# Two transfers on GpSimd's queue behind the first pair of its sums, in a gated two-layer MLP with seven-product matmuls

## Chip, cores and metric

One core of one Trainium2 chip. The metric is device time in microseconds (us), the median of several executions; lower is better. "Set" is a quarter of the tokens (1024 of 4096); the kernel works through four sets one after the other. A "chunk" is 128 of the 2048 columns of the hidden layer; each of the sums S1 to S4 of g has eight chunks.

## The reference

```python
x: 16 x 256 x 512, w1: 512 x 4096, w2: 2048 x 512      # float32
h = x @ w1
gate, value = np.split(h, 2, axis=-1)
h = np.maximum(gate, 0) * value
return (h @ w2).astype(np.float32)
```

## The kernel before

Both matmuls are done as seven products of 2x2 blocks instead of eight. That needs sums of the operands: T1 to T4 of the weights, S1 to S4 of x and of the gated hidden layer g.

Accumulating and casting transfers are issued by GpSimd, each with one helper (cut, comments added):

```python
SUMS = (("S1", "A21", "A22", SUB), ("S2", "S1", "A11", SUB), ("S4", "A12", "S2", ADD), ("S3", "A11", "A21", SUB))

def add_w2(m, v):
    nc.gpsimd.dma_start(out=V[m], in_=V[v], accum_op=ADD)

def cast_x(s):                       # x of set s to 16 bits, in DRAM; DMA transposes read it later
    nc.gpsimd.dma_start(out=x16[s], in_=x2[s * SET:(s + 1) * SET, :])

def g_sum(eng, go, n, h0, h1):       # chunks h0 to h1 of sum n, by engine eng
    for m, i0, i1, op in SUMS:
        if m == n:
            eng.tensor_tensor(go[n][:, h0:h1], go[i0][:, h0:h1], go[i1][:, h0:h1], op=op)
```

GpSimd's work in the first set, in its order (cut, comments added):

```python
for t in TURNS:
    w1_one(nc.gpsimd, 12, 4, *t)
    if t[0] == "T2":
        add_w2("T1", "B12")
add_w2("T3", "B22")
add_w2("T2", "T1")                   # must wait until T1 has landed
cast_x(1)
...
    if n == "P2" and s == 0 and jb in (11, 13, 15):
        h = jb - 11                  # 0, 2, 4
        if h == 4:
            add_w2("T4", "T2")       # must wait until T2 has landed
        for m in ("S1", "S3")[:2 - h // 4]:
            g_sum(nc.gpsimd, go, m, h, h + 2)
```

So GpSimd makes two pairs (S1 and S3 of chunks 0 to 1, then 2 to 3) and one last sum, S1 of chunks 4 to 5. What is left is VectorE's after the set's last block (cut):

```python
        if s == 0:
            g_sum(nc.vector, go, "S1", 6, 8)
            for m in ("S2", "S4"):
                for h in (0, NHC // 2):
                    g_sum(nc.vector, go, m, h, h + NHC // 2)
            g_sum(nc.vector, go, "S3", NHC // 2, NHC)
```

TensorE reads them right after, in the products P5 (S1), P6 (S2), P3 (S4), P7 (S3). VectorE's next work in its order is two evictions each of P3 and P7 (an eviction takes a finished product out of the memory in which TensorE adds up), the four sums of the next set's x, eight sums of w1 and then the evictions of the second half.

Of the kernel before, what the change touches and what calls it, by code (L numbers as in the profile page):

```python
# [29 lines left out]
@with_exitstack  # L30
def kernel(ctx: ExitStack, tc: tile.TileContext, x, w1, w2, out):






    nc = tc.nc
    x2 = x.flatten_outer_dims()
    out2 = out.flatten_outer_dims()  # L40
    flagpool = ctx.enter_context(tc.tile_pool(name="flagpool", bufs=1))
    flag = flagpool.tile([1, 1], dt.int32, name="flag")
    with ExitStack() as fast:
        unfit = fast_way(fast, tc, x2, w1, w2, out2, flag)
    with tc.If(unfit > 0, label="general"):
        with ExitStack() as general:
            general_way(general, tc, x2, w1, w2, out2)
# [52 lines left out]
def fast_way(ctx, tc, x2, w1, w2, out2, flag):  # L100
# [54 lines left out]
    def w1_ops(eng, jb, n):  # L155
        for t in TURNS:
            w1_one(eng, jb, n, *t)

    def w1_one(eng, jb, n, m, a, b, o):
        eng.tensor_tensor(W(m, jb, n), W(a, jb, n), W(b, jb, n), op=o)  # L160

    def add_w2(m, v):
        nc.gpsimd.dma_start(out=V[m], in_=V[v], accum_op=ADD)
# [12 lines left out]
    def x_tiles():  # L176
        o = {f"A{h}": xpool.tile([P, 4, TH], F16, name=f"x_A{h}") for h in (1, 2)}
        for h in (1, 2):
            for k in (1, 2):
                o[f"A{h}{k}"] = o[f"A{h}"][:, 2 * k - 2:2 * k]  # L180
        for n in ("S1", "S2", "S3", "S4"):
            o[n] = xpool.tile([P, 2, TH], F16, name=f"x_{n}")
        return o
# [88 lines left out]
    def g_sum(eng, go, n, h0, h1):  # L272
# [3 lines that stand above are left out]
# [69 lines left out]
    def advance(stream, n):  # L345
        for _ in range(n):
            if stream is None or next(stream, 0) == 0:
                return
# [5 lines left out]
    def fetch_w2(i):  # L354
        ks, n = slice(i // 2 * NHC, i // 2 * NHC + NHC), i % 2
        nc.gpsimd.dma_start(out=w2_h[n][:, ks], in_=w2_v[:, ks, n * HALF:(n + 1) * HALF])

    def cast_x(s):
        nc.gpsimd.dma_start(out=x16[s], in_=x2[s * SET:(s + 1) * SET, :])

    def g_tiles():
        g = gpool.tile([P, NJ, SET], F16, name="g")
        gs = {n: gpool.tile([P, NHC, TH], F16, name=f"g_{n}") for n in ("S1", "S2", "S3", "S4")}
        return g, g_ops(g, gs)
# [21 lines left out]
    def turn_by_dma(s, o, h):  # L386
        for k in range(2):
            nc.sync.dma_start_transpose(out=o[f"A{h + 1}{k + 1}"], in_=x16[s][h * TH:(h + 1) * TH, k * 256:k * 256 + 256])
# [7 lines left out]
    def fetch_rows(s, q):  # L396
        rows[s, q] = xpool.tile([P, 2, D], F16, name=f"xn{q % 2}")
        nc.sync.dma_start(out=rows[s, q], in_=x16[s][q * 256:(q + 1) * 256].rearrange("(b p) d -> p b d", p=P))
# [50 lines left out]
    def x_sum(o):  # L449
        n, i0, i1, op = sums.pop(0)  # L450
        nc.vector.tensor_tensor(o[n], o[i0], o[i1], op=op)
# [64 lines left out]
    for s in range(NS):  # L516
        if s:
            g, go = g_tiles()
        first = NPLAIN if s == 0 else 0
        blocks = {jb: Block(xo, g, jb) for jb in range(first, NJ)}  # L520
        if s == 0:
            blocks[first] = lead
        plan = {jb * PERIOD + at: (jb, n) for jb in blocks for n, at in SLOT.items() if (s, jb, n) != (0, first, "P1")}
        last = NJ * PERIOD
        stream = mm2_stream(s, go)
        if s == 0:
            w1_ops(nc.gpsimd, 4, 2)
            fetch_w2(0)
            fetch_w2(1)
            w1_ops(nc.gpsimd, 6, 2)  # L530
            fetch_w2(2)
            fetch_w2(3)
            w1_ops(nc.gpsimd, 8, 2)
            w1_ops(nc.gpsimd, 10, 2)
            for to, v in ((V["T1"], V["B11"]), (v_12, w2_h[1]), (V["T4"], V["B21"])):
                nc.sync.dma_start(out=to, in_=v)
            for t in TURNS:
                w1_one(nc.gpsimd, 12, 4, *t)
                if t[0] == "T2":
                    add_w2("T1", "B12")  # L540
            add_w2("T3", "B22")
            add_w2("T2", "T1")
            cast_x(1)
        for at in range(first * PERIOD, last + PERIOD):
            if at in plan:
                jb, n = plan[at]
                if n == "P1" and s and jb in (4, 8):
                    fetch_rows(s, 1 + jb // 4)
                if n == "P2" and s == 0 and jb in (11, 13, 15):
                    h = jb - 11  # L550
                    if h == 4:
                        add_w2("T4", "T2")
                    for m in ("S1", "S3")[:2 - h // 4]:
                        g_sum(nc.gpsimd, go, m, h, h + 2)
                getattr(blocks[jb], n)()
                ended = jb - (n == "P7") if n == "P7" or (n, jb) == ("P4", NJ - 1) else -1
                if ended in blocks:
                    blocks[ended].finish()
                if n == "P5":
                    for f in LOOKS.get((s, jb), ()):  # L560
                        f()
                if ended >= 0 and s:
                    if ended < NHC:
                        g_sum(nc.gpsimd, go, "S3", ended, ended + 1)
                        if s == 1 and ended in (1, 4):
                            cast_x(2 + ended // 4)
                    elif ended < NJ - BY_DVE:
                        for m in ("S1", "S2", "S4"):
                            g_sum(nc.gpsimd, go, m, ended - NHC, ended - NHC + 1)
            elif at >= last:  # L570
                advance(stream, 4)
            else:
                advance(prev, 4)
# [6 lines that stand above are left out]
        else:  # L580
            for m in ("S1", "S2", "S4"):
                g_sum(nc.vector, go, m, NHC - BY_DVE, NHC)
        done = 20
        if s + 1 < NS:
            xo = x_tiles()
            for h in range(2):
                turn_by_dma(s + 1, xo, h)
            for q in range(2):
                fetch_rows(s + 1, q)
            advance(stream, 100)  # L590
            sums = list(SUMS)
            for _ in SUMS:
                x_sum(xo)
            if s == 0:
                w1_ops(nc.vector, 0, 2)
                w1_ops(nc.vector, 2, 2)
            advance(stream, MM2 - TAIL - 100 - done)
        else:
            advance(stream, MM2)
        prev = stream  # L600
# [29 lines left out]
```

## Time and profile before

| | before |
|---|---|
| time, median of 3 | 311.59 us (311.24 to 311.88) |
| profiled span | 309.5 us |
| TensorE busy | 301.5 us (97%) |
| GpSimd busy | 148.0 us (48%) |
| TensorE idle outside start and end | 0.74 us by the records, all between 66 and 74 us |

The "busy" of an engine is the time in its instructions. In the rows in order of time that follow, the columns are start, duration, engine, line, operation, output and inputs, count, and in brackets the idle time of the engine just before and what ended it. TensorE's matmul ends are modelled and overlap the next start, so gaps are best taken from starts. The lines that carry the reading stand in the prediction.

### The profile page before, as it was taken

What the parts mean: (1) busy time and instruction counts of PE and PEld (TensorE: products, weight loads), DVE (VectorE), ACT (ScalarE), POOL (GpSimd) and SP (SyncE); (2) the same over time, 40 slices, a digit from 0 to 9 for tenths busy, and PEclk for the clock granted to TensorE, in tenths of its full rate; (3) what the DMA queues carried; (4) which work ended last, traced back from release to release, by engine and by line L of the source; (5) the groups of instructions that cost most, each with busy time, mean ns of one, the idle gap of its engine ahead of it and who ended that gap; (6) DMA issues with size and microseconds to landing.
All of it is one profiled execution on the core that took longest, in us unless ns stands there. A gap on an engine that the chain in (4) does not pass through costs nothing.

```text
span 309.5 us, 5081 instructions
## 1 busy us (share of the span) xinstructions
PE 301.5 (97%) x1859; PEld 181.9 (59%) x1859; DVE 217.0 (70%) x330; ACT 188.8 (61%) x450; POOL 148.0 (48%) x135
## 2 busy tenths in 40 slices
PE   7999999999999999999999999999999999999994
PEld 4554444578854444478874444458884444447883
DVE  1477888898548888884338888886526888888401
ACT  3357766547577667648847667656857666673230
POOL 5779996950003437992001435995000434899000
PEclk9999999999999999999999999999999999999999
DMA  7999979998314370055221010028311101000113
GB/s 250 203 203 204 224 198 215 204 120 238 120 68 102 71 169 0 3 95 159 87 102 37 34 34 2 0 48 156 140 71 68 34 2 34 0 2 0 69 68 140
DMA packets 33450, 30.74 MB, mean 99 GB/s; under 512 B 13873, under 2 KB 27953, under 8 KB 33201
## 3 DMA queue, kind: packets, MB, share of 16 engines
q0 software_dynamic: 10704, 11.54, 23.0%
q1 hardware_dynamic: 22576, 18.75, 20.6%
q8 instruction: 15, 0.25, 0.3%
q10 hardware_dynamic: 144, 0.13, 0.1%
q14 instruction: 11, 0.08, 0.1%
HBM read 24.12 MB, written 11.53 MB: 115 GB/s over the span
## 4 chain that ended last, share of the span: by engine, by line
PE 92%; DVE 2%; ACT 2%; DMA 1%; issue 1%; SPq 0%; DVEq 0%
PE Y L202 25%; PE X L202 16%; PE W L202 16%; PE Y L286 13%; PE W L286 8%; PE X L286 8%; PE X L259 2%; PE W L259 2%; DMA g<-in_w_dram 1%; DVE g_S L275 1%; ACT x_A L377 0%; ACT v L264 0%; ACT x_A L384 0%; PE W L375 0%; DVE g L241 0%
## 5 line engine op out<-in xcount | busy, mean ns | idle before, releaser
L275 POOL TENSOR_TENSOR g_S<-g 128x512 f16<-128x512 f16 (+1 forms) x47 | 60.0, 1300 | 125.3 <-DVE g L241 123.3
L202 PEld LDWEIGHTS <-wt 128*128 128x128 f16 x480 | 47.0, 98 | 55.3 <-issue 0.6
L202 PE MATMUL Y<-x_S,wt 128*128 128x512 f16 x240 | 71.4, 379 | 0.0
L202 PE MATMUL X<-x_A,wr 128*128 128x512 f16 x240 | 71.4, 379 | 0.0
L202 PEld LDWEIGHTS <-wr 128*128 128x128 f16 x360 | 35.2, 98 | 40.7 <-issue 0.2
L229 DVE SCALAR_TENSOR_TENSOR cc<-W,pu 128x512 f32<-128x512 f32 x60 | 41.5, 692 | 23.6 <-ACT pu L223 23.5
L209 ACT COPY Y<-X 128x512 f32<-128x512 f32 x60 | 34.2, 571 | 37.5 <-PE X L202 37.0
L286 PEld LDWEIGHTS <-g_S 128*128 128x128 f16 x512 | 49.9, 98 | 7.0 <-DVE g_S L275 1.3
L235 DVE SCALAR_TENSOR_TENSOR cc<-Y,pu 128x512 f32<-128x512 f32 x60 | 41.5, 691 | 6.4 <-PE Y L202 0.4
L223 ACT ACTIVATE pu<-Y 128x512 f32<-128x512 f32 x60 | 35.8, 597 | 14.2 <-PE Y L202 14.2
L230 DVE SCALAR_TENSOR_TENSOR g<-X,cc 128x512 f16<-128x512 f32 x60 | 41.5, 691 | 2.3
L286 PEld LDWEIGHTS <-g 128*128 128x128 f16 x384 | 37.5, 98 | 8.2
L241 DVE SCALAR_TENSOR_TENSOR g<-Y,cc 128x512 f16<-128x512 f32 x60 | 40.9, 681 | 1.8 <-PE Y L202 1.8
L216 ACT ACTIVATE pu<-W 128x512 f32<-128x512 f32 x60 | 36.1, 602 | 0.3 <-PE W L202 0.3
L202 PE MATMUL Y<-x_A,wt 128*128 128x512 f16 x120 | 35.7, 379 | 0.1
L202 PE MATMUL W<-x_S,wr 128*128 128x512 f16 x120 | 35.7, 379 | 0.0
L202 PE MATMUL W<-x_S,wt 128*128 128x512 f16 x120 | 35.7, 379 | 0.0
L286 PE MATMUL X<-w,g 128*128 128x256 f16 x256 | 31.2, 273 | 0.0
L286 PE MATMUL Y<-v,g_S 128*128 128x256 f16 x256 | 30.7, 273 | 0.4 <-DVE g_S L275 0.4
L316 DVE SCALAR_TENSOR_TENSOR o<-W,pv 128x256 f32<-128x256 f32 x16 | 6.8, 423 | 30.3 <-PE W L286 30.3
L275 POOL TENSOR_TENSOR g_S<-g,g_S 128x512 f16<-128x512 f16 x18 | 21.8, 1211 | 1.4
L275 POOL TENSOR_TENSOR g_S<-g_S,g 128x512 f16<-128x512 f16 x18 | 21.4, 1187 | 1.4
(69 smaller groups left out, 294.7 us busy)
## 6 DMA issues: line engine op xcount, KB each, us to landing
out_dram<-o SPq DMA_DIRECT2D x16, 256.0 KB, 2.1
out_dram<-pv SPq DMA_DIRECT2D x15, 256.0 KB, 2.0
x<-in_x_dram POOLq DMA_DIRECT2D x3, 1024.0 KB, 8.1
xn<-x SPq DMA_DIRECT2D x12, 256.0 KB, 3.3
wr<-in_w_dram POOLq DMA_DIRECT2D x4, 512.0 KB, 14.4
w<-in_w_dram POOLq DMA_DIRECT2D x4, 512.0 KB, 11.9
wr<-in_w_dram POOLq DMA_DIRECT2D x6, 256.0 KB, 8.4
g_S<-in_x_dram SPq DMA_DIRECT2D x2, 512.0 KB, 4.6
```

The lines of the kernel that those rows point to most:

```text
L202: nc.tensor.matmul(ps, W(wn, self.jb)[:, b], self.xo[xn][:, b, :], start=fresh and b == 0, stop=b == 1, skip_group_check=True)
L209: nc.scalar.copy(out=self.Y, in_=self.X)
L216: nc.scalar.activation(self.p5, self.W, COPY, scale=GS)
L223: nc.scalar.activation(self.u2, self.Y, COPY, scale=-GS)
L229: nc.vector.scalar_tensor_tensor(out=self.c12, in0=self.W, scalar=GS, in1=self.u2, op0=MULT, op1=ADD)
L230: nc.vector.scalar_tensor_tensor(out=self.g[:, self.jb, :TH], in0=self.X, scalar=0.0, in1=self.c12, op0=MAX, op1=MULT)
L235: nc.vector.scalar_tensor_tensor(out=self.c22, in0=self.Y, scalar=-GS, in1=self.p5, op0=MULT, op1=ADD)
L241: nc.vector.scalar_tensor_tensor(out=self.g[:, self.jb, TH:], in0=self.Y, scalar=0.0, in1=self.c22, op0=MAX, op1=MULT)
L259: nc.tensor.matmul(ps[:, ts], W(name, self.jb)[:, e % 2], a[:, e, ts], start=e == 0, stop=e == 3, skip_group_check=True)
L275: eng.tensor_tensor(go[n][:, h0:h1], go[i0][:, h0:h1], go[i1][:, h0:h1], op=op)
L286: nc.tensor.matmul(ps, go[gn][:, k, b * P:(b + 1) * P], V[vn][:, k, :], start=fresh and k == 0, stop=k == NHC - 1, skip_group_check=True)
L316: nc.vector.scalar_tensor_tensor(out=d["o1"][:, HALF:], in0=d["W"], scalar=1 / GS, in1=d["pu"][:, 1], op0=MULT, op1=ADD)
```

## The change

Its intent: GpSimd stood waiting for T1 to land, ahead of the T2 transfer, while sums that it could have made were ready. T2 and the cast of x go behind the first pair of sums.

```diff
             add_w2("T3", "B22")
-            add_w2("T2", "T1")
-            cast_x(1)
...
                     for m in ("S1", "S3")[:2 - h // 4]:
                         g_sum(nc.gpsimd, go, m, h, h + 2)
+                    if h == 0:
+                        add_w2("T2", "T1")
+                        cast_x(1)
```

## The prediction

> **What bounds the kernel now.** I read the page's busy shares first, then the row of tenths, the chain that ended last inside the stretch that the change touches, and last the instructions of GpSimd, VectorE and TensorE there in order of time.
>
> The page, parts 1 and 2:
>
> ```profile
> PE 301.5 (97%) x1859; PEld 181.9 (59%) x1859; DVE 217.0 (70%) x330; ACT 188.8 (61%) x450; POOL 148.0 (48%) x135
> ...
> PE   7999999999999999999999999999999999999994
> ```
>
> TensorE is busy 301.5 of 309.5 us, so whatever GpSimd does, all that can be won is the 8 us in which TensorE is idle. Most of that is the first and the last slice (the table of stretches has 2.46 us in the first 10 us, 3.9 us in the last 29), which this change doesn't touch. The same table, cut finer between 62 and 78 us (columns: stretch, length, then busy us and count for PE, PEld, DVE, ACT, POOL, then clock, DMA share, GB/s), has the only other hole of any size:
>
> ```profile
> 64.00:66.00 2.00, 2.00 (x21) 1.80 (x19) 2.00 (x1) 1.01 (x3) 1.82 (x1) 1.00 0.97 168
> 66.00:70.00 4.00, 3.61 (x34) 3.01 (x32) 4.00 (x5) 2.73 (x7) 0.00 (x0) 1.00 1.43 149
> 70.00:74.00 4.00, 3.65 (x34) 3.04 (x33) 3.23 (x5) 3.23 (x7) 0.00 (x0) 1.00 0.95 185
> 74.00:78.00 4.00, 4.00 (x39) 3.57 (x38) 3.65 (x7) 2.78 (x6) 0.00 (x0) 1.00 0.90 321
> ```
>
> Note also "2.00 (x1)" of VectorE in 64 to 66: one instruction fills it. The chain of waits there leaves TensorE for VectorE's sums (L275) just after the first set's last block:
>
> ```profile
> 63.11 0.70 DVE g L241
> ...
> 66.44 1.00 issue
> 67.43 3.50 DVE g_S L275 x3
> 70.93 0.05 issue
> 70.97 1.48 PE W L286 x12
> ```
>
> VectorE's and TensorE's instructions in order of time say which sums, and when TensorE stood still for them:
>
> ```profile
> 63.84 2.54 DVE L275 TENSOR_TENSOR g_S<-g 128x1024 f16<-128x1024 f16 x1
> 66.30 2.35 DVE L275 TENSOR_TENSOR g_S<-g_S,g 128x2048 f16<-128x2048 f16 x2
> 68.57 2.35 DVE L275 TENSOR_TENSOR g_S<-g,g_S 128x2048 f16<-128x2048 f16 x2
> 70.84 1.21 DVE L275 TENSOR_TENSOR g_S<-g 128x2048 f16<-128x2048 f16 x1
> ```
>
> ```profile
> 67.71 0.60 PE L286 MATMUL Y<-v,g_S 128*128 128x256 f16 x4
> 68.70 1.49 PE L286 MATMUL Y<-v,g_S 128*128 128x256 f16 x12 [0.39 <-DVE g_S L275]
> 70.03 0.60 PE L286 MATMUL W<-w,g_S 128*128 128x256 f16 x4
> 70.97 1.48 PE L286 MATMUL W<-w,g_S 128*128 128x256 f16 x12 [0.35 <-DVE g_S L275]
> ```
>
> The four rows of sums are S1 of chunks 6 to 7, then S2, S4 (two halves each) and the upper half of S3. TensorE has done four of eight steps of a group when the half that VectorE hasn't finished stops it. GpSimd's rows say why the first sum took 2.54 us:
>
> ```profile
> 49.70 0.89 POOL L163 DMA_DIRECT2D v<-w  x1 [0.25 <-issue]
> 53.04 0.85 POOL L163 DMA_DIRECT2D v<-v_T  x1 [2.44 <-DMA v_T<-w]
> 53.58 0.85 POOL L359 DMA_DIRECT2D x<-in_x_dram  x1
> 54.13 8.69 POOL L275 TENSOR_TENSOR g_S<-g 128x1024 f16<-128x1024 f16 x4
> 62.45 1.22 POOL L163 DMA_DIRECT2D v_T<-v  x1
> 63.06 2.75 POOL L275 TENSOR_TENSOR g_S<-g 128x1024 f16<-128x1024 f16 x1
> ```
>
> GpSimd's last sum (S1 of chunks 4 to 5) runs from 63.06 to 65.81, and VectorE's sum of the same size, begun at 63.84, ends only at 66.38, 0.57 us after it. GpSimd is that late because it stood 2.44 us ahead of the T2 transfer (the row with v<-v_T), waiting for T1 to land.
>
> **What the Trainium skill says.** "SBUF — State Buffer", section "SBUF: two separate sides", calls the SBUF port pair shared by VectorE and GpSimd "an exclusive lock, not a bandwidth split", taken by the first for its whole instruction, which a VectorE instruction with two SBUF inputs also needs. The trace agrees: VectorE's sums of 128x1024 take 0.69 us with the pair free (137.74 us; x_S at 74.58 is 0.68) and 2.54 us here, while the PSUM-reading instructions keep 0.69 us beside a running GpSimd. "DMA: Bandwidth & Descriptors", section "Rules for kernel authors", has accumulating and casting transfers issued from GpSimd, so the two moved transfers must stay in GpSimd's order; its section "Anatomy of one DMA — SWDGE (gpsimd) path" puts any semaphore wait on the issuing sequencer. The 2.44 us in which GpSimd issued no sum agrees. "GPSIMD Engine Reference", section "Engine selection", gives about a factor of 2 against VectorE for two inputs; here 2.1 us start to start against 0.69 is 3.
>
> **The change part by part.** Nothing is added or removed, so no engine's busy time should move by itself except VectorE's blocked sum. Two transfers go behind two sums.
>
> 1. The wait for T1. After the T3 issue GpSimd used to be free at 49.70 + 0.54 = 50.24 us (issues start 0.54 apart: 53.04, 53.58, 54.13). The first pair needs g of chunks 0, 1, 8 and 9; VectorE finishes chunk 9 at about 47.5 (its L241 row at 46.86). So the pair starts at 50.25, and at (62.45 - 54.13)/4 = 2.08 us each it ends at 54.41. T1 has landed by 53.0; the wait of 2.44 us is gone, filled with 4.16 us of work.
> 2. T2 is issued at 54.41 instead of 53.04 (+1.37), the cast of x at 54.95 instead of 53.58 (+1.37).
> 3. The second pair (chunks 2 and 3) runs from 55.50 to 59.66; its chunk 11 is done at 53.7. T4 must wait for T2, which takes 5.5 us to land: 54.41 + 5.5 = 59.9. So T4 starts at 59.9, not 62.45, with a new wait of about 0.25 us. The last sum starts at 60.5 (chunk 13 is done at 59.62) and ends at 62.6 to 62.9, that is 3 us earlier than 65.81.
> 4. VectorE reaches its first sum at 63.84 as before, as that hangs on the last block, but finds the ports free: 0.69 instead of 2.54 us. Its next sums start at 64.57, 65.70, 66.84, 67.97 and 69.11 (1.135 apart, as now). The second half of S2 ends at 66.9, that of S4 at 69.2.
> 5. TensorE. Its steps are 0.1092 us apart (1.75 us per 16). The second half of S2 is wanted at 67.71 + 4 x 0.109 = 68.15 and was got at 68.70: 0.55 lost. That of S4 was wanted at 70.03 + 0.44 = 70.47 and got at 70.97: 0.50 lost. In the new order they are wanted at 68.15 and 69.90, and are there 1.2 and 0.7 us before. All 1.05 us is won. Check by length: from 62.91 to 72.30 are 76 steps, 8.30 us of work in 9.39, so 1.09 us. The row of idle shows 0.39 + 0.35 only, because the ends of matmuls are modelled to overlap; I take the starts.
> 6. The price is x of the second set. The cast took 9.8 us to land, at 63.4, when the first DMA transpose starts (63.43). It now lands at about 64.8. The last transpose, begun at 70.7, landed at 74.3, so now at about 75.7. VectorE's x sums, at 74.58 now, wait till then (it would be free at about 73.6): a new wait of about 2 us, with its weight sums ending near 81.3 instead of 80.25. TensorE wants x_S first at 85.83 - 1.05 = 84.8, and the next VectorE eviction falls due near 81.1. Nothing of it lies on the path.
>
> Sum: -1.05 to -1.09 us, from there to the end TensorE runs without a gap that could absorb it. 311.59 - 1.07 = 310.5 us, -0.35%.
>
> **Rivals.** (a) The wait only moves: T4's wait for T2 replaces T2's wait for T1, GpSimd's last sum stays late, no gain, 311.6. For it: T4 is bound to T2's landing. Against: that is 0.25 us by the sum above, and the last sum may end as late as 64.5 before S4 is late again, 1.6 us or more in hand. If T2 landed 2 us later than thought, half of the gain would go. (b) The delayed cast holds up the second set: 312 to 313. For it: the cast's landing is what releases the transposes, with nothing in hand there. Against: about 8 us in hand at x_S. (c) Part gain: only the S2 stop goes and S4's stays, because VectorE's sums are themselves a series of 5.5 us; 311.0. Against: 0.7 us in hand at S4. (d) More than the sum: nothing else that TensorE waits for in the middle hangs on GpSimd; I see no second gain.
>
> **Range and chances.** The three runs of before lie within 0.64 us, so noise on a median is some 0.3 us. The sum is 310.5; rival (c) or part of (a) pulls up, little pulls down: 310.1 to 311.3. A gain of 2% would be 6.2 us, more than TensorE's whole idle time outside its start and end, and a loss of that size would need x_S over 14 us late. Faster 0.01, within 2% 0.98, slower 0.01.
>
> **What would show it.** GpSimd: four rows between 50 and 60 us without the 2.44 us wait, the last sum ended before 63.8. VectorE: first sum at 63.84 of about 0.7 us; a new wait of about 2 us for the transposes ahead of the x sums. TensorE: no idle charged to VectorE's sums, stretches 66 to 70 and 70 to 74 at 4.00. I'd be wrong if the first sum on VectorE still took 2.5 us (steps 1 to 3 failed), if it took 0.7 but TensorE stopped all the same (step 5), or if TensorE stood at the start of the second set near 84 us (step 6).

## The result, and the profile after

| | before | changed |
|---|---|---|
| median of 4 | 311.41 us (311.00 to 311.88) | 310.77 us (310.68 to 310.91) |
| ratio, 95% interval | 1 | 0.9979 (0.9962 to 0.9997) |
| TensorE busy of the span | 301.5 of 309.5 us | 301.5 of 309.1 us |

A ratio here is the mean time of one kernel's fast runs over that of the other's of the same rounds, so it isn't quite the ratio of the medians. The gain is 0.64 us by the medians, 0.2%: inside the predicted range, but only about 60% of the 1.07 us that the sum gave.

GpSimd in the changed kernel, in order of time:

```profile
49.65 1.18 POOL L163 DMA_DIRECT2D v<-w  x1
50.29 4.79 POOL L275 TENSOR_TENSOR g_S<-g 128x1024 f16<-128x1024 f16 x2
54.44 1.46 POOL L163 DMA_DIRECT2D v<-v_T  x1
55.03 1.43 POOL L359 DMA_DIRECT2D x<-in_x_dram  x1
55.58 5.11 POOL L275 TENSOR_TENSOR g_S<-g 128x1024 f16<-128x1024 f16 x2
60.77 0.88 POOL L163 DMA_DIRECT2D v_T<-v  x1
61.39 2.42 POOL L275 TENSOR_TENSOR g_S<-g 128x1024 f16<-128x1024 f16 x1
```

No wait is charged any more, and the last sum ends at 63.81 instead of 65.81. One wait is there all the same: by the starts two such sums take 4.16 us, so GpSimd was through with the second pair at about 59.7, but T4, which needs T2, went out at 60.77, when T2 landed (6.0 us from issue to landing). The recorded 5.11 us of the pair covers that wait: where the cast stands behind the same pair (a run below), the pair's record is 5.11 us too and the cast goes out 4.15 us after its start. VectorE's sums in the changed kernel:

```profile
64.08 0.69 DVE L275 TENSOR_TENSOR g_S<-g 128x1024 f16<-128x1024 f16 x1
64.69 2.35 DVE L275 TENSOR_TENSOR g_S<-g_S,g 128x2048 f16<-128x2048 f16 x2
66.96 2.35 DVE L275 TENSOR_TENSOR g_S<-g,g_S 128x2048 f16<-128x2048 f16 x2
...
74.69 0.69 DVE L451 TENSOR_TENSOR x_S<-x_A 128x1024 f16<-128x1024 f16 x1 [0.87 <-DMA x_A<-x]
```

The first takes 0.69 instead of 2.54 us. The price is in the last row: a new wait of 0.87 us for the DMA transposes of x. TensorE's rows and the chain of waits there:

```profile
63.16 3.22 PE L286 MATMUL X<-w,g 128*128 128x256 f16 x28
66.21 1.91 PE L286 MATMUL W<-v_T,g_S 128*128 128x256 f16 x16
67.96 1.91 PE L286 MATMUL Y<-v,g_S 128*128 128x256 f16 x16
69.71 1.91 PE L286 MATMUL W<-w,g_S 128*128 128x256 f16 x16
...
84.55 0.59 PE L202 MATMUL X<-x_A,wr 128*128 128x512 f16 x2
```

```profile
66.38 1.75 PE W L286 x16
68.12 1.75 PE Y L286 x16
69.87 1.75 PE W L286 x16
```

The groups of four and twelve are whole groups of sixteen again, without idle time, and VectorE has left the chain. Three landmarks split the span. The 28 steps (the first row above: TensorE's last work before it needs the sums of g) begin 62.91 us (before) and 63.16 us (changed) from the start; from there to the second set's first step (85.39 and 84.55) it is 22.48 and 21.39 us; from there to the span's end 224.1 and 224.55. The middle part won 1.09 us, as worked out. The changed kernel lost 0.25 us of it before the change acts (its lead-in is already 0.24 us late at 10 us), and 0.44 us at the end, between TensorE's last group and the span's end. One profile can't say whether those two are chance.

### The profile page after: what moved, and what is told of

Its sections match the earlier page's. It is cut to its first block, busy times and chain, and to the rows that moved or that the text cites. A ratio compares the mean times of both kernels' runs of the same rounds, so it can differ in the third digit from the quotient of the medians.

```text
span 309.1 us, 5081 instructions
## 1 busy us (share of the span) xinstructions
PE 301.5 (98%) x1859; PEld 182.2 (59%) x1859; DVE 215.8 (70%) x330; ACT 188.8 (61%) x450; POOL 148.1 (48%) x135
## 4 chain that ended last, share of the span: by engine, by line
PE 94%; DMA 2%; ACT 1%; DVE 1%; issue 0%; SPq 0%
PE Y L202 25%; PE X L202 16%; PE W L202 16%; PE Y L286 14%; PE W L286 9%; PE X L286 9%; PE X L259 2%; PE W L259 2%; DMA g<-in_w_dram 2%; ACT v L264 0%; ACT x_A L384 0%; DVE cc L229 0%; DVE g L230 0%; DVE x_A L377 0%; ACT wr L391 0%
## 5 line engine op out<-in xcount | busy, mean ns | idle before, releaser
L275 POOL TENSOR_TENSOR g_S<-g 128x512 f16<-128x512 f16 (+1 forms) x47 | 60.9, 1329 | 126.5 <-DVE g L241 124.5
```

## The experiments

I measured each run by its ratio to the kernel before (same chip, same rounds) and by the landmarks in its profile. L is the start of the 28 steps, P the end of GpSimd's last sum of two inputs in the first set, X the second set's first step. The experiments ran on three chips: the four rows from "change again" on one, the next four on a second, the last four on a third. Diffs are against the changed kernel where the heading doesn't say "before".

| kernel | L | P | X | X - L | ratio, 95% interval |
|---|---|---|---|---|---|
| before | 62.91 | 65.81 | 85.39 | 22.48 | 1 |
| changed | 63.16 | 63.81 | 84.55 | 21.39 | 0.9979 (0.9962 to 0.9997) |
| change again | 63.42 | 63.65 | 84.82 | 21.40 | 0.9985 (0.9972 to 0.9999) |
| only T2 moved | 63.31 | 68.04 | 88.74 | 25.43 | 1.0049 (1.0029 to 1.0069) |
| only the cast moved | 63.84 | 65.98 | 85.56 | 21.72 | 1.0005 (0.9991 to 1.0020) |
| change, one idle sum more | 63.43 | 65.82 | 85.40 | 21.97 | 1.0007 (0.9992 to 1.0022) |
| change, three idle fills more | 62.96 | 63.61 | 84.35 | 21.39 | 0.9980 (0.9967 to 0.9994) |
| before, last sum to VectorE | 63.38 | 62.93 | 84.78 | 21.40 | 0.9981 (0.9967 to 0.9994) |
| change, cast one pair later | 63.53 | 63.66 | 85.27 | 21.74 | 1.0004 (0.9990 to 1.0017) |
| change, cast last | 62.91 | 63.72 | 88.83 | 25.92 | 1.0111 (1.0095 to 1.0126) |
| before again | 62.87 | 66.11 | 85.69 | 22.82 | 0.9998 (0.9984 to 1.0013) |
| before, third profile | 63.05 | 65.84 | 85.42 | 22.37 | one run |
| before, TensorE later | 64.02 | 65.40 | 85.41 | 21.39 | 0.9997 (0.9982 to 1.0012) |
| change, TensorE later | 63.94 | 64.54 | 85.33 | 21.39 | 0.9999 (0.9983 to 1.0015) |

Theory A: the gain is that VectorE's first sum no longer finds the shared ports taken by GpSimd's last sum. Rivals: B, the result of GpSimd's last sum was late as data; C, the gain comes from moving the transfers themselves; N, part of the gain is given back at start or end.

**The change again**, unaltered.

> The changed kernel unaltered, in more rounds. Theory A (ports: the gain is VectorE's first sum no longer held up by GpSimd's last one): TensorE's stretch from the first step of the 28 ahead of the seven products (62.9 us in the profile of before) to its last group's start is 1.1 us shorter than before, and the time 0.9 to 1.1 us lower, ratio about 0.9967. Rival N (part of the gain is given back at the start or the end of the program by later transfers): the stretch is 1.1 us shorter but the time only 0.6 us lower again, with the lead-in and the tail longer in this profile as in the first one (+0.25 and +0.45).

The stretch X - L came out at 21.40, the ratio at 0.9985: 0.47 us won of 311.6. The lead-in was long again, but the end (309.0 - 84.82 = 224.2) was not. N as stated, an end made longer by the change, doesn't hold; the small gain does.

**Only T2 behind the pair.**

```diff
             add_w2("T3", "B22")
+            cast_x(1)
...
                     if h == 0:
                         add_w2("T2", "T1")
-                        cast_x(1)
```

> Only T2 goes behind the first pair; the cast of x goes ahead of it. Theory A: what counts is the end of GpSimd's last sum. The cast (issued at about 50.2, 10 us to land) is now ahead of T2 in the same transfers' queue, so T2 lands later than 60.5, at 61 to 62, T4 waits for it, the last sum ends at 64.5 to 65.3, VectorE's first sum takes 1 to 2 us, and TensorE loses 0 to 0.4 us at S4: gain 0.7 to 1.1 us. If T2 is not held up by the cast, last sum at 63 and the full gain. Rival C (the gain comes from x being moved out of the way of the first sums): no gain, as x is now early.

It is slower than the kernel before. GpSimd's row of the T4 issue, then TensorE's two stops:

```profile
64.79 0.87 POOL L163 DMA_DIRECT2D v_T<-v  x1 [4.11 <-DMA v<-v_T]
```

```profile
68.10 1.48 PE L286 MATMUL W<-v_T,g_S 128*128 128x256 f16 x12 [1.13 <-POOL g_S L275]
...
77.38 1.92 PE L286 MATMUL Y<-v_T,g 128*128 128x256 f16 x16 [2.52 <-DMA v_T<-v]
```

T2, issued at 54.95 behind the cast, landed at about 64.8, 9.6 us from issue to landing, against 6.0 us in the changed kernel. I had expected 61 to 62. T4 waited for it, so the last sum ended at 68.04; now its data are late (rival B's wait, which the kernel before didn't have), and T4 itself landed so late that TensorE stopped 2.52 us more. The profiled run is the slowest of its six (314.80; the others from 312.36), so the landings vary. What follows: T2 must stay ahead of the cast, and that is why both had to move.

**Only the cast behind the pair.**

```diff
             add_w2("T3", "B22")
+            add_w2("T2", "T1")
...
                     if h == 0:
-                        add_w2("T2", "T1")
                         cast_x(1)
```

> Only the cast goes behind the first pair; T2 stays ahead, so GpSimd waits for T1 (2.4 us) again. Theory A: GpSimd's last sum ends at about 65.8 as before, VectorE's first sum takes 2.5 us, TensorE loses 1.0 us: time as before (ratio 1.000 +- 0.001), and x lands about 4 us later than before without harm. Rival C: the gain of the change (ratio 0.997).

No gain (1.0005), so C falls: the later x alone wins nothing. P is 65.98, as before. But TensorE lost only 21.72 - 21.39 = 0.33 us, not 1.0, with the same P. In this profile it had begun the 28 steps at 63.84, 0.93 us later than in the first profile of before. That is what led to the last four runs.

**One idle sum more.**

```diff
+                    if h == 4:
+                        nc.gpsimd.tensor_tensor(go["S4"][:, 6:8], go["A21"][:, 4:6], go["A22"][:, 4:6], op=SUB)
```

Nobody reads what it writes; VectorE overwrites it when it makes S4, and its first sum and S2 wait for nothing of it.

> The change plus one more GpSimd sum of two inputs of the size of the last one, right behind it, into a place that VectorE overwrites later and that its first sum doesn't touch. Theory A: GpSimd's ports are taken till about 65.9, VectorE's first sum takes about 2.4 us and TensorE loses about 1 us: the whole gain gone, ratio to before 0.999 to 1.001. Rival B (VectorE's S2 waited for the result of GpSimd's last sum; earlier result, earlier S2): nothing that VectorE's S1 or S2 needs is later, so the gain stays: ratio 0.997.

The ratio is 1.0007: the gain is gone. GpSimd's row and VectorE's first sum:

```profile
63.41 2.41 POOL L557 TENSOR_TENSOR g_S<-g 128x1024 f16<-128x1024 f16 x1
```

```profile
64.36 2.02 DVE L275 TENSOR_TENSOR g_S<-g 128x1024 f16<-128x1024 f16 x1
```

VectorE's sum ends 0.56 us after a GpSimd sum with which it shares no data. B falls for the kernel before; A holds. In "only T2 moved" VectorE's wait for GpSimd's data stood as idle time ahead of its row (2.01 us); here there is none, and the row itself is longer.

**Three idle fills more.** The same place, without reading:

```diff
+                    if h == 4:
+                        for _ in range(3):
+                            nc.gpsimd.memset(go["S4"][:, 6:8], 0.0)
```

> As the run with the extra sum, but with three fills with zero (no reading) in its place. Theory A, as the Trainium skill states it for two-input VectorE instructions (only against a GpSimd instruction that reads SBUF): VectorE's first sum takes about 0.7 us although GpSimd is busy, TensorE loses nothing, ratio to before 0.997. Rival A2 (any GpSimd instruction takes the ports): VectorE's first sum is held up till the fills end and part or all of the gain is gone.

```profile
63.26 3.26 POOL L558 MEMSET g_S<- 128x1024 f16 x3
```

```profile
63.88 0.69 DVE L275 TENSOR_TENSOR g_S<-g 128x1024 f16<-128x1024 f16 x1
```

GpSimd is busy till 66.5, VectorE's sum takes its 0.69 us all the same, the gain stays (0.9980). It is GpSimd's sum, which reads two inputs, that blocks, not a busy GpSimd; A2 falls. An instruction with one input wasn't tried.

**The kernel before, its last GpSimd sum given to VectorE.**

```diff
-                    for m in ("S1", "S3")[:2 - h // 4]:
+                    for m in ("S1", "S3") if h < 4 else ():
                         g_sum(nc.gpsimd, go, m, h, h + 2)
...
-            g_sum(nc.vector, go, "S1", 6, 8)
+            g_sum(nc.vector, go, "S1", 4, 8)
```

> The kernel before with its order of transfers, but GpSimd's last sum made by VectorE (its first sum twice as large). Theory A: no GpSimd sum runs beside VectorE's; its first sum takes 1.2 us instead of 2.54, S4's second half ends about 0.55 us later than with the change, at about 69.7 against 69.9 wanted: gain 0.9 to 1.1 us, ratio 0.997, with nothing of the change in it. Rival (the gain hangs on the transfers' new order): no gain.

GpSimd waits for T1 here as before (2.22 us in this profile), and yet the stretch is 21.40 and the ratio 0.9981, as with the change: VectorE's sum, twice as large, takes 1.23 us, less than one of half that size took blocked. The wait for T1 cost nothing by itself; what cost was the meeting of the two sums, to which it led. This version is as fast as the change, not faster.

**The cast later still.** One pair later:

```diff
                     if h == 0:
                         add_w2("T2", "T1")
+                    if h == 2:
                         cast_x(1)
```

> The change with the cast one pair later still (issued at about 60). Theory A and slack of x: x lands at 69 to 70, transposes end at 77 to 78, VectorE waits 4 us for them, weight sums end near 84; TensorE wants x_S at 84 to 85. No loss, or under 0.3 us: ratio to before 0.997 to 0.998. Rival (a later x is what takes back part of the gain): 0.5 us or more slower than the change.

A miss: 1.0004. By the times about 0.7 us, the whole gain, is gone; the profile's stretch shows 21.74 - 21.39 = 0.35 us of it, and the rest lies within the intervals. The x sums began at 77.67, and weight sums ran to 83.35. TensorE then stood, by the profile for VectorE's eviction:

```profile
84.40 1.03 PE L286 MATMUL Y<-v_T,g 128*128 128x256 f16 x8 [0.18 <-DVE pv L321]
```

The bound is not the use of x_S. It is the evictions that stand behind the x sums in VectorE's order, which TensorE needs 1.3 us earlier (in the changed kernel 83.68 for the row above, 84.98 for the first use of x_S).

**The cast last**, the same with `h == 4`.

> The change with the cast behind GpSimd's last sum (issued at about 63.5). x lands at 72 to 73, transposes end near 81, x sums near 84, weight sums near 87; VectorE's evictions in between queue up behind them. By the slack of x that I worked out, TensorE must now stand at the start of the second set: 1 to 4 us lost against the change, ratio to before 1.000 to 1.01.

1.0111, or 3.5 us slower than before. The same row now has 3.57 us:

```profile
87.17 1.87 PE L286 MATMUL Y<-v_T,g 128*128 128x256 f16 x8 [3.57 <-DVE pv L321]
```

The eight steps took 1.87 instead of 1.04 us; the granted clock (TensorE's, 1 is full speed) was 0.67 between 85 and 90 us. In this one profile the part from the second set's first step to TensorE's last group was 218.43 us, against 217.78 or 217.79 in all others, so the stop cost more than its length.

**Where the rest of the gain is.** Over the rows above there is a pattern. Where TensorE stops at the sums (before, only the cast, idle sum), X - P is 85.39 - 65.81 = 19.58, 85.56 - 65.98 = 19.58, 85.40 - 65.82 = 19.58: X hangs on GpSimd's clock alone (an engine's clock means here when it gets to the sums, not the granted clock). Where it doesn't stop (changed, again, fills, last sum to VectorE), X - L is 21.39 or 21.40: X hangs on TensorE's clock alone. Theory H: the stop is a race of two clocks, P - L - 1.81 us (21.39 - 19.58), and the first profile of before had TensorE early. Rival F: the stop is fixed at 1.09 us and the smaller measured gain is noise. The remaining runs tell H from F.

The kernel before again, for its profile and for what a comparison with itself gives:

> The kernel before, unaltered, against itself: what the timing can tell, ratio 1.000 +- 0.0015. Theory H (a race: in the kernel before, the end of the first set hangs on GpSimd's clock and not on TensorE's, so a late start of TensorE is absorbed; the first profile of before had TensorE 0.5 us earlier than the typical run, which made its stall look larger than it is in the mean): the 28 steps begin at any time from 62.9 to 63.9, but the second set's first step at 85.3 to 85.6 whatever they do. Rival F (a fixed stall of 1.09 us, the gain hidden by noise): the second set begins 22.48 us after the 28 steps again.

And once more for its profile alone:

> The kernel before once more, for its profile alone. Theory H: the second set's first step at 85.3 to 85.6 us, whenever the 28 steps begin; rival F: 22.48 us after them.

Against itself the ratio is 0.9998 (0.9984 to 1.0013). X - P is 85.69 - 66.11 = 19.58 and 85.42 - 65.84 = 19.58, to the last digit. L was 62.87 and 63.05, so early again and not spread from 62.9 to 63.9 as I expected; X - L was 22.82 and 22.37, not 22.48, and the 85.69 lies just outside the 85.3 to 85.6 I gave. The rule in P holds; these two profiles alone don't show that a later TensorE is absorbed.

So TensorE was made late on purpose. The kernel before with four more matmul steps in the first set, overwritten at once, so the result is unchanged:

```diff
         def P1(self):
             self.X = psx.tile([P, TH], F32, name="X", tag="X")
-            self.mm("P1", self.X, True)
+            for _ in range(2 if self.twice else 1):
+                self.mm("P1", self.X, True)
...
+                blocks[jb].twice = s == 0 and jb in (8, 9)
```

> The kernel before with four more matmul steps of 512 in TensorE's row in the first set (0.216 us each, 0.86 us in all, results overwritten). Theory H: GpSimd's last sum ends at 65.8 to 66.0 as before, TensorE comes to the sums at 64.0 to 64.7, little or no stall is left (stretch 21.4 to 21.6 us), and the time rises only 0.1 to 0.5 us over before, ratio 1.0003 to 1.0015. Rival F: the full 0.86 us, ratio 1.0028, stretch 22.5.

The changed kernel with the same four steps:

> The changed kernel with the same four more steps. Both theories: 0.86 us slower than the change, as it has no stall to absorb them (stretch 21.4 us). Theory H: then the change is worth 0 to 0.2 us against the other kernel with the four steps. Rival F: worth 1.1 us.

The kernel before took 0.86 us more work on its bounding engine at no cost: 0.9997 (F asked for 1.0028, outside the interval). L is 64.02, X 85.41, the stretch 21.39; the stop is gone. GpSimd was early in this profile (P 65.40, not the expected 65.8 to 66.0); with a P of 65.9 the rule would leave a stop of 65.9 - 64.02 - 1.81 = 0.07 us, so nearly none either way. VectorE's first sum met only the last part of GpSimd's:

```profile
64.94 1.02 DVE L277 TENSOR_TENSOR g_S<-g 128x1024 f16<-128x1024 f16 x1
```

The changed kernel lost its whole gain to the same steps (0.9999; from 0.9979 and 0.9985 that is 0.4 to 0.6 us, where both theories asked for 0.86; the difference lies within the intervals), and the two kernels with the steps are equal, 311.42 and 311.40 us. F falls, H stands: the change is worth only as much as TensorE is ahead of GpSimd.

Where does TensorE's clock come from? In 11 of the 14 profiles the chain of waits begins with the first transfer of w1: it took 4.62 us in the first profile of before and 5.56 in the run where only the cast moved; TensorE's first real step came at 7.21 and 8.14, L at 62.91 and 63.84, all three 0.93 or 0.94 apart. This is the start-up of a transfer that no version here touches. Over the 14 profiles L lies between 62.87 and 63.84, mean 63.2 (0.86 taken off in the two with added steps). By chip, in the order of the table, it lies at 63.31 to 63.84, 62.91 to 63.53 and 62.87 to 63.16, so part of the spread may belong to the chips and not to the runs; three or four profiles of each can't tell. With P near 65.9 (mean of the three profiles of before) the rule gives a mean gain of 65.9 - 63.2 - 1.8 = 0.9 us. The four measured ratios of versions with the full effect (0.9979, 0.9985, 0.9980, 0.9981) give 0.5 to 0.65 us. The difference of about 0.3 us lies inside the intervals; whether it is chance or whether L is later in unprofiled runs stays open.

## Why the prediction was right or wrong

- What bounds: right. TensorE's busy time is 301.5 us in both, and only the hole at 66 to 74 us closed.
- Step 1, the wait for T1 is filled with the first pair: right (50.29 to 54.44).
- Steps 2 and 3: T2 at 54.44 was right to 0.03 us. The last sum was to end at 62.6 to 62.9 and ended at 63.81, as T4's wait for T2 was about 1.0 us and not 0.25 (60.77 - 59.7, see above): T2 took 6.0 us to land, not 5.5, and the sum counted these from the start of its row, while in "only T2 moved" T4 was let go 9.84 us after T2's row began, for 9.6 us to landing. It was in time for VectorE at 64.08 by only 0.27 us. A GpSimd end up to about 64.5 was called harmless; the profile didn't need that room.
- Step 4, VectorE's first sum in 0.69 us: right. That the meeting with GpSimd's sum made it long is shown by the idle sum, the fills and the sum given to VectorE; the ports themselves no run shows, but all three agree with that reading.
- Step 5 is the term that was mis-sized. The 1.05 to 1.09 us is exactly what this profile's stretch won, but I subtracted it from a median as if it were a constant. It is P - L - 1.81, and L differs by up to a microsecond between profiles (0.3 to 0.6 us on one chip), mostly with the first transfer. By the times the gain is 0.5 to 0.65 us.
- Step 6: x was late by 2.8 us (transposes from 66.20, 11.1 us after the cast's issue, where 9.8 was assumed), but the four transposes then were issued in 6.30 instead of 8.55 us, so VectorE waited 0.87 us, not 2. Nothing of it reached TensorE: right. The "8 us in hand at x_S" of rival (b), however, was wrong: with x sums 3 us later than in the changed kernel 0.35 us was lost already, because evictions stand behind them in VectorE's order.
- Rival (c) didn't come, and (a) only in part: T4's wait for T2 took about 1.0 us back of GpSimd's gain, but TensorE stopped neither at S2 nor at S4. With the cast ahead of T2, T4's wait came to 4.11 us.

## What to carry to other kernels

A stall in one profile is the difference of two clocks, so before subtracting it from the time, ask what sets each and how far either moves from run to run and from chip to chip; delaying the waiting engine on purpose shows at once whether a stall is fixed or a race. An engine with plenty of idle time can still cost, if its instruction takes ports that the critical engine needs at that moment; give the sum away or time it otherwise, as filling its waits is only a means. In an in-order queue, look at what stands behind the work you delay: here evictions behind the x sums, and one transfer behind a larger one.

## What the Trainium skill lacked or had wrong

- "SBUF — State Buffer", "SBUF: two separate sides": right in both halves. A two-input VectorE sum was blocked until 0.56 us after a GpSimd sum's end (2.02 and 2.54 us instead of 0.69), and not at all by GpSimd fills that read nothing (0.69). That the blocked instruction appears in the profile as a longer one and not as a wait is not said there.
- "GPSIMD Engine Reference", "Engine selection": about 2x against VectorE for two inputs; these 16-bit sums took 2.08 us start to start against 0.69, a factor of 3.
- "DMA: Bandwidth & Descriptors", "Anatomy of one DMA — SWDGE (gpsimd) path": its fit (2.0 us plus bytes over 436 GB/s) would give an estimate of 3.2 us for an accumulating transfer of 512 KB. T2 took 5.5 and 6.0 us, and 9.6 behind the cast; T4 took 6.0, 9.4 and 12.5. The page doesn't say there whether the fit is meant for accumulating transfers or for a busy queue.
- None of the pages read gives the spread of a transfer from run to run: the same first load took 4.54 to 5.56 us over three chips, 4.61 to 5.16 on one of them; between two profiles (4.62 and 5.56) TensorE was 0.93 us later, more than the change won.
